# A DRAIN on GpSimd ahead of the last gather of a mixture-of-experts layer

## The chip, the cores and the metric

The kernel runs on one core of a Trainium2 chip. The metric is the device time of one execution in microseconds (us). The core has five engines with an instruction queue each: TensorE (PE in the rows; PEld is its weight load), VectorE (DVE), ScalarE (ACT), GpSimd (POOL) and SyncE (SP), and 16 DMA engines that they share. A q behind an engine's name in a row (POOLq, SPq) means an instruction that the engine's queue handles by itself, such as a wait on a semaphore, a branch or a DRAIN. Such instructions are not counted as busy time.

## The reference, cut to what matters

One layer: a gated linear attention over 512 tokens with 256 tokens of context, then a mixture of 16 experts with two experts for each token, then a norm.

```python
h2 = _modulate(_rmsnorm(x, norm2_g[i]), sh2, sc2).reshape(n_lat, D_MODEL)
f = _moe(h2, w_router, b_router, w_gate_e[i], w_up_e[i], w_down_e[i])
x = x + g2 * f.reshape(bsz, t, D_MODEL)
return _rmsnorm(x, final_g)
...
def _moe(h, w_router, b_router, w1, w3, w2):   # gates: the two best experts of the best group
    for e in range(N_EXPERTS):
        he = jax.nn.silu(h @ w1[e]) * (h @ w3[e])
        out = out + gates[:, e:e + 1] * (he @ w2[e])
    return out
```

## The kernel before

All weights are float32 and are read once, in transfers of 1 MB that SyncE issues. The attention comes first; its result x1 (512 rows of 1024) is written to a DRAM buffer `accd`, and the normed rows to `h2d`. Then the experts run one after another, in an order that the routing sets at run time. For each expert GpSimd gathers the rows of its tokens from `h2d` (an indirect DMA, `gather`, L1107), TensorE multiplies them with the expert's weights, VectorE scales the result into `y`, and GpSimd adds `y` to the rows of `accd` (an indirect DMA that accumulates, `scatter_add`, L1111). A tile whose expert may get at most 64 tokens is a `Part`, which lays 128 // w pieces of a row over the partitions.

The tail is written out by hand, from L1418 on, and its order is the order of the code on all five engines. `p_` is the expert before the last (index NE - 2), `q_` the last.

- L1425, L1426: the down product of `p_` and its scatter. This scatter is the last but one that the program may issue; the loop at L1492 has further ones, but it runs only where an expert has more rows than its tile holds, and in the profiled execution its branch is taken past it.
- L1427: the final norm's gain is laid out (TensorE, ScalarE; nothing on GpSimd). L1428, L1429: the up and gate products of `q_`.
- L1430 to L1436: SyncE loads the last weights and, by `finish_load` (L1343), the finished rows of `accd` into four tiles `y`, which needs the scatter of `p_` to have landed.
- L1437, `late_rows`: GpSimd gathers from `accd` (L1379 through L1107) the rows of the tokens of the last expert into `t.z`. It waits for the same scatter.
- L1440, `finish_half`: for two tiles at a time, the squares on ScalarE (L1346), the multiplication with the gain (L1352: tiles 0 and 2 on GpSimd, 1 and 3 on VectorE), the scaling on VectorE (L1356), and the store (L1357).
- L1442 to L1446: the down product of `q_`, its addition to the gathered rows (L1382), their norm, and `late_store`: GpSimd writes those rows straight into the output (L1394), over what `finish` stored.

Then comes what the framework adds (L1491 and L1492, and L1530, the end of the program): each engine waits for the semaphores of all DMAs, and two rounds of a barrier follow, in each of which every engine runs a DRAIN and GpSimd gathers the arrivals and lets the others go. Of what is executed before the change, only the opening barrier (L1523) and the closing ones (L1530) hold DRAINs.

GpSimd issues DMAs of two kinds in the program: plain ones (rows named DMA_DIRECT2D) and indirect ones (DMA_INDIRECT). Its instructions around the change are the two scatters at L1111, the gather at L1107, the two multiplications at L1352 and the store at L1394.

Of the kernel before, what the change touches and what calls it, by code (L numbers as in the profile page):

```python
# [32 lines left out]
def dit_kernel(ctx: ExitStack, tc: tile.TileContext, I, out):  # L33
    nc = tc.nc
    V, S, G, PE = nc.vector, nc.scalar, nc.gpsimd, nc.tensor
# [10 lines left out]
    def bank(p=None):  # L46
        p = p or pa
        return p.tile([P, 512], F32, tag="bk", name="bk")
# [633 lines left out]
    def load_unit(u, e, s, hs=None):  # L682
        t = u[s] if s in u else free.pop(0)
        if t is None:
            t = stg.tile([P, 2048], F32, tag="st", name="st")
        if s < 4:
            w, kk, v = I[("w_gate_e", "w_up_e")[s % 2]], 4, s // 2
        else:
            w, kk, v = I["w_down_e"], 2, s - 4
        w = w[0, e] if isinstance(e, int) else w[0, bass.ds(e, 1)].rearrange("a k n -> (a k) n")  # L690
        h = range(kk) if hs is None else hs
        d = nc.sync.dma_start(t.rearrange("p (k n) -> p k n", k=kk)[:, h.start:h.stop],
                              w.rearrange("(k p) n -> p k n", p=P)[:, kk * v + h.start:kk * v + h.stop])
        if len(dmas) >= 3 and not isinstance(e, int):
            back = 2 if hs is not None or len(dmas) >= 88 else 3
            tc.add_manual_dep(d.ins, dmas[-back].ins.name, mybir.DependencyInfo(mybir.DependencyClass.Sync, mybir.DependencyReason.DATA), reason="queue depth")
        dmas.append(d)
        u[s] = t
# [628 lines left out]
    def lay(name, src):  # L1327
        A = P // tiles[-1][2]
        for a in range(A):
            q, n = slice(P // A * a, P // A * (a + 1)), D // A  # L1330
            S.copy(fin[name][q, 0:n], src[q, a * n:a * n + n])

    def finish_g():
        for a in range(2):
            sl = slice(a * 512, a * 512 + 512)
            pt = bank()
            PE.matmul(pt, one, fin["row"][:, sl], start=True, stop=True)
            S.copy(fin["g"][:, sl], pt)
        lay("h", fin["g"])

    def finish_load(ts=range(4)):
        for t in ts:
            nc.sync.dma_start(fin["y"][t], accd[t * P:(t + 1) * P, :])  # L1343
# [15 lines left out]
    def finish_half(t):  # L1359
        squares(t)  # L1360
        finish_mul(t)
        if t == 0:
            finish_mul(1)
        squares(t + 1)
        finish_rsqrt(t)
        finish(t)
        finish(t + 1)
# [9 lines left out]
    def late_rows(t):  # L1377
        t.z = xbuf()[:, 0:t.n]
        gather(t.z, parts(accd, t.A), t.idx, t.A * T)  # L1379

    def late_add(t):
        V.tensor_add(t.z, t.z, t.y)  # L1382

    def late_square(t):
        S.activation(mo.tile([P, 512], BF16, tag="ohx", name="jk3", bufs=NO)[:, 0:t.n], t.z, AF.Square, accum_out=lss)

    def late_out(t):
        pt = bank(pb)
        PE.matmul(pt[:, 0:1], SELP, lss, start=True, stop=True)
        rsqrt(lrs, pt[:, 0:1], 1, 1.0 / D, "x")  # L1390
        V.scalar_tensor_tensor(t.z, t.z, lrs, fin["h"][:, 0:t.n], op0=OP.mult, op1=OP.mult)

    def late_store(t):
        G.indirect_dma_start(out=parts(out[0], t.A), out_offset=bass.IndirectOffsetOnAxis(ap=t.idx, axis=0), in_=t.z, in_offset=None,  # L1394
                             bounds_check=t.A * T - 1, oob_is_err=False)
# [24 lines left out]
    with tc.manual_schedule(engines=tail):  # L1420
        p_, q_ = ex[NE - 2:]
        p, q = p_.tls[0], q_.tls[0]
        p.late = mo.tile([P, D], F32, tag="t4", name="y", bufs=NY)[:, 0:p.n]
        q.late = fin["y15"][:, 0:q.n]
        p_.down(wts[NE - 2])  # L1425
        p_.scatter()  # L1426
        finish_g()  # L1427
        q_.up(wts[NE - 1], "a")  # L1428
        q_.up(wts[NE - 1], "b")  # L1429
        for c in "uFab":  # L1430
            if c == "F":
                finish_load()
            elif c in "0123":
                finish_load([int(c)])
            else:
                load_unit(wts[NE - 1], regs[NE - 1], {"u": 4}.get(c, 5), {"a": range(1), "b": range(1, 2)}.get(c))  # L1436
        late_rows(q)  # L1437
        q_.turn()
        S.preload_act_table_set("natural_log_exp_and_others")
        for h in range(2):  # L1440
            finish_half(2 * h)
        q_.down(wts[NE - 1])  # L1442
        late_add(q)
        late_square(q)
        late_out(q)
        late_store(q)  # L1446
# [87 lines left out]
```

## Time and profile before

| | |
|---|---|
| median of 3 runs | 674.66 us (674.36 to 675.53) |
| the profiled execution | 677.96 us |
| its span, first to last instruction | 676.2 us |
| what lies around the span | 1.76 us |
| PE, DVE, ACT, POOL busy | 617.7, 465.6, 303.6, 101.9 us |
| DMA | 170.92 MB, mean 253 GB/s |

The profile records one execution by itself, 3.3 us longer than the median of the runs. Its times count from the first instruction of the span. TensorE is busy 91% of the span, but the last six microseconds or so hold no busy engine at all; what stands there is only in the rows of the queues.

### The profile page before, as it was taken

How to read it: one execution, taken by the hardware profiler on the slowest of the kernel's cores; microseconds unless marked ns; L12 is line 12 of the kernel's file. 1: busy time of each engine (PE TensorE's matmuls, PEld its weight loads, DVE VectorE, ACT ScalarE, POOL GpSimd, SP SyncE). 2: the span in 40 equal slices, each digit the busy share in tenths (PEclk: the TensorE clock that was granted, in tenths of full speed). 3: DMA queues.
4: the chain of work that ended last, by engine and by line, in shares of the span. 5: the costliest groups of instructions: out<-in, count | busy, mean ns of one | idle time of the engine just before them, and what ended most of it. 6: DMA issues, size and time to landing. Idle time of an engine off the chain costs nothing. (4 is left out here: it accounts for less than half of the span.)

```text
span 676.2 us, 11367 instructions
## 1 busy us (share of the span) xinstructions
PE 617.7 (91%) x4260; PEld 417.3 (62%) x4260; DVE 465.6 (69%) x994; ACT 303.6 (45%) x513; POOL 101.9 (15%) x104
## 2 busy tenths in 40 slices
PE   3999999999999999999988899999999999999650
PEld 3777577767878878778773664545465667654210
DVE  5776499669958934653685796563776789999332
ACT  6334397276241416523431554323453567762240
POOL 3030000010100010104002143011212222330130
PEclk9999999999999999999989899999999999999755
DMA  8995562210336754297748899999999999999882
GB/s 277 340 353 174 194 241 63 64 64 3 127 93 223 246 188 174 88 360 251 298 143 296 329 300 369 329 337 315 328 342 371 334 348 367 373 385 337 260 317 111
DMA packets 79163, 170.92 MB, mean 253 GB/s; under 512 B 6325, under 2 KB 16875, under 8 KB 78210
## 3 DMA queue, kind: packets, MB, share of 16 engines
q1 hardware_dynamic: 71760, 156.26, 65.3%
q0 software_dynamic: 5248, 10.68, 6.8%
q10 hardware_dynamic: 2098, 3.24, 1.6%
q8 instruction: 34, 0.56, 0.3%
q14 instruction: 23, 0.19, 0.1%
HBM read 158.90 MB, written 13.09 MB: 254 GB/s over the span
## 5 line engine op out<-in xcount | busy, mean ns | idle before, releaser
L51 PE MATMUL bk<-wh,fh 128*128 128x512 f32 (+3 forms) x276 | 111.7, 412 | 1.2 <-ACT fh L56 1.2
L52 PE MATMUL bk<-wl,fh 128*128 128x512 f32 (+3 forms) x276 | 110.7, 403 | 0.0
L53 PE MATMUL bk<-wh,fl 128*128 128x512 f32 (+3 forms) x276 | 109.2, 400 | 0.0
L282 DVE TENSOR_TENSOR wl<-st,wh 128x512 fp32r<-128x512 f32 x60 | 39.9, 686 | 39.1 <-ACT wh L281 37.8
L1111 POOL DMA_INDIRECT accd<-y,gix x17 | 41.0, 2410 | 169.7 <-DVE y L1171 78.6
L56 ACT CAST wh<-su 128x1024 fp32r<-128x1024 f32 x45 | 46.8, 1049 | 42.7 <-PE bk L53 41.6
L51 PEld LDWEIGHTS bk<-wh,fh 128*128 128x128 f32 (+3 forms) x276 | 50.4, 184 | 24.0 <-issue 5.9
L281 ACT CAST wh<-st 128x512 fp32r<-128x512 f32 x60 | 35.9, 621 | 61.0 <-PE bk L53 50.8
L57 DVE TENSOR_TENSOR wl<-su,wh 128x1024 fp32r<-128x1024 f32 x45 | 54.5, 1221 | 12.3 <-ACT wh L56 9.3
L52 PEld LDWEIGHTS bk<-wl,fh 128*128 128x128 f32 (+3 forms) x276 | 50.8, 184 | 15.2 <-issue 2.4
L53 PEld LDWEIGHTS bk<-wh,fl 128*128 128x128 f32 (+3 forms) x276 | 50.5, 183 | 13.4 <-issue 1.2
L1207 PE MATMUL bk<-su,xg 128*32 128x256 f32 (+1 forms) x248 | 42.7, 503 | 5.2 <-DMA su<-in_w_up_e_dram 3.8
L1107 POOL DMA_INDIRECT xg<-h2d,gix x17 | 21.2, 1249 | 86.6 <-DMA h2d<-xg 48.9
L56 ACT CAST fx<-su 128x1024 fp32r<-128x1024 f32 x21 | 22.0, 1048 | 26.1 <-PE bk L53 25.5
L57 DVE TENSOR_TENSOR fx<-su,fx 128x1024 fp32r<-128x1024 f32 x21 | 25.7, 1222 | 11.0 <-ACT fx L56 10.8
L51 PE MATMUL bk<-fx,fh 128*128 128x512 f32 (+3 forms) x68 | 28.5, 419 | 0.1
L52 PE MATMUL bk<-fx,fh 128*128 128x512 f32 (+3 forms) x68 | 27.6, 405 | 0.8 <-DVE fx L57 0.8
L53 PE MATMUL bk<-fx,fl 128*128 128x512 f32 (+3 forms) x68 | 26.9, 396 | 0.2 <-DVE fl L57 0.2
L1207 PEld LDWEIGHTS bk<-su,xg 128*32 128x32 f32 (+1 forms) x248 | 12.1, 126 | 23.7 <-issue 16.6
L1207 PE MATMUL bk<-su,he 128*64 128x512 f32 (+1 forms) x136 | 23.1, 555 | 3.9 <-DVE he L1224 2.1
L250 POOL DMA_DIRECT2D mrd<-mrow x8 | 3.8, 484 | 130.5 <-DVE mrow L248 130.5
L1238 DVE SCALAR_TENSOR_TENSOR y<-bk,gsl,g1b 64x512 f32<-64x512 f32 (+1 forms) x16 | 10.9, 681 | 14.6 <-PE bk L1207 14.5
(478 smaller groups left out, 1318.5 us busy)
## 6 DMA issues: line engine op xcount, KB each, us to landing
su<-in_w_up_e_dram SPq DMA_DIRECT2D x23, 1024.0 KB, 9.3
su<-in_w_down_e_dram SPq DMA_DIRECT2D x21, 1024.0 KB, 8.2
su<-in_w_gate_e_dram SPq DMA_DIRECT2D x19, 1024.0 KB, 7.9
st<-in_gla_w_in_dram SPq DMA_DIRECT2D x10, 1024.0 KB, 5.3
QQ<-in_w_mod_dram SPq DMA_DIRECT2D x5, 1024.0 KB, 6.4
st<-in_w_gate_e_dram SPq DMA_DIRECT2D x5, 1024.0 KB, 7.7
st<-in_w_up_e_dram SPq DMA_DIRECT2D x5, 1024.0 KB, 7.5
B<-in_w_mod_dram SPq DMA_DIRECT2D x4, 1024.0 KB, 4.8
```

Of the source, the lines that this page charges most:

```text
L51: PE.matmul(o, ah, bh, start=first, stop=False)
L52: PE.matmul(o, ah, bl, start=False, stop=False)
L53: return PE.matmul(o, al, bh, start=False, stop=last)
L56: S.copy(hi, full)
L57: return V.tensor_sub(lo, full, hi.bitcast(F32))
L250: G.dma_start(mrd[4 * h_ + c4:4 * h_ + c4 + 1, :], mrow[32 * c4:32 * c4 + 1, :])
L281: S.copy(w[0][:, k], st[:, k])
L282: mark[0] = V.tensor_sub(w[1][:, k], st[:, k], w[0][:, k].bitcast(F32))
L1107: G.indirect_dma_start(out=xg, out_offset=None, in_=src, in_offset=bass.IndirectOffsetOnAxis(ap=idx, axis=0), bounds_check=n - 1, oob_is_e ...
L1111: G.indirect_dma_start(out=dst, out_offset=bass.IndirectOffsetOnAxis(ap=idx, axis=0), in_=y, in_offset=None, bounds_check=n - 1, oob_is_er ...
L1207: PE.matmul(o[s.w * a:s.w * a + s.w], l, r(a), start=first, stop=last, tile_position=(0, s.w * a))
L1238: s.mark = V.scalar_tensor_tensor(y[q], s.py[q], s.gs[q], g2b[q, a * s.n:a * s.n + s.n], op0=OP.mult, op1=OP.mult)
```

## The change

One line: a DRAIN instruction on GpSimd's queue, between the scatter of the expert before the last and the gather for the last expert. The DRAIN carries no wait on a semaphore and sets none. In the built program it is the only instruction that is added; nothing is removed or moved on any engine, and every other instruction waits for the same counts as before. The lines below it move down by one: L1427 is the DRAIN afterwards, the closing barrier is L1531, the branch past the loop L1493.

```diff
         p_.down(wts[NE - 2])
         p_.scatter()
+        G.drain()
         finish_g()
         q_.up(wts[NE - 1], "a")
         q_.up(wts[NE - 1], "b")
```

## Rows read from the trace of the kernel before

**Rows 1.** Busy time of each engine in four stretches at the end (from:to in us, length, busy us and number of instructions of each engine, TensorE's granted clock, the share of the DMA engines that was busy, GB/s).
```profile
639.80:647.40 7.60, 3.50 (x40) 1.48 (x36) 0.00 (x0) 0.00 (x0) 0.00 (x0) 0.72 0.91 297
647.40:656.90 9.50, 6.60 (x50) 2.04 (x42) 3.35 (x6) 5.52 (x10) 6.33 (x3) 0.50 0.89 340
666.90:669.60 2.70, 0.00 (x0) 0.00 (x0) 0.00 (x0) 0.00 (x0) 0.00 (x0) 0.50 0.08 24
669.60:675.40 5.80, 0.00 (x0) 0.00 (x0) 0.00 (x0) 0.00 (x0) 0.00 (x0) 0.50 0.00 0
```

**Rows 2.** The instructions of the program's last line, L1530 (engine, operation, count: shortest/median/longest in ns, start of the first and of the last in us).
```profile
L1530 POOLq EVENT_SEMAPHORE  x4: 17/17/17, 675.4 to 676.1; - x4
L1530 SPq DRAIN  x3: 7/7/13, 669.4 to 675.6; - x3
L1530 POOLq DRAIN  x3: 46/105/5703, 669.6 to 675.9; - x3
L1530 ACTq DRAIN  x2: 8/8/8, 669.5 to 675.6; - x2
L1530 DVEq DRAIN  x2: 10/14/17, 669.8 to 675.6; - x2
L1530 PEldq DRAIN  x2: 8/8/8, 670.0 to 675.7; - x2
```

**Rows 3.** Waits of SyncE's queue from 640 us on (who waited, for whom: us in total, times, longest).
```profile
SPq L1530 <- PEq L1530: 6.6, 2, 6.1
SPq L1343 <- DMA accd<-y,gix: 4.0, 1, 4.0
```

**Rows 4.** The program's opening, L1523, on GpSimd's queue (columns as in rows 2).
```profile
L1523 POOLq INC_SWDGE_SEM  x1: 27/27/27, 0.1 to 0.1; - x1
...
L1523 POOLq DRAIN  x1: 188/188/188, 0.3 to 0.3; - x1
```

**Rows 5.** The branch past the loop, L1492, on GpSimd's queue (columns as in rows 2).
```profile
L1492 POOLq INC_SWDGE_SEM  x1: 1575/1575/1575, 666.5 to 666.5; - x1
```

**Rows 6.** GpSimd's instructions over the whole span, by line: those that issue a DMA (count, busy us, mean ns, idle time before them and what ended it).
```profile
L1111 POOL DMA_INDIRECT accd<-y,gix x17 | 41.0, 2410 | 169.7 <-DVE y L1171 78.6 <-DVE y L1238 39.2 <-DMA accd<-y,gix 15.7
L1107 POOL DMA_INDIRECT xg<-h2d,gix x17 | 21.2, 1249 | 86.6 <-DMA h2d<-xg 48.9 <-DVE pis L1010 19.8 <-PE bk L1220 12.0
...
L234 POOL DMA_DIRECT2D mrow<-in_b_mod_dram x8 | 3.9, 506 | 33.9 <-DVE mrow L232 33.8
L250 POOL DMA_DIRECT2D mrd<-mrow x8 | 3.8, 484 | 130.5 <-DVE mrow L248 130.5
L324 POOL DMA_DIRECT2D F<-in_gla_b_gate_dram x6 | 3.1, 518 | 0.0
L323 POOL DMA_DIRECT2D F<-in_gla_w_gate_b_dram x6 | 2.9, 487 | 34.5 <-DVE F L326 33.0 <-DMA F<-in_gla_w_gate_b_dram 1.3 <-issue 0.2
...
L121 POOL DMA_DIRECT2D wga<-in_gla_w_gate_a_dram x2 | 1.9, 946 | 0.0
...
L1107 POOL DMA_INDIRECT xg<-accd,gix x1 | 1.1, 1078 | 7.6 <-DMA st<-in_w_up_e_dram 7.6
L1394 POOL DMA_INDIRECT out_dram<-xg,gix x1 | 1.1, 1057 | 9.5 <-DVE xg L1391 9.5
...
L79 POOL DMA_DIRECT2D raw<-in_b_mod_dram x1 | 0.7, 694 | 0.9 <-POOLq L1523 0.9
L80 POOL DMA_DIRECT2D raw<-in_norm_g_dram x1 | 0.6, 590 | 0.0
...
L81 POOL DMA_DIRECT2D raw<-in_gla_norm_g_dram x1 | 0.5, 523 | 0.0
```

**Rows 7.** GpSimd's instructions in order of time in the tail (start us, us, what; in brackets the idle time before, and what ended it).
```profile
638.23 1.55 POOL L1111 DMA_INDIRECT accd<-y,gix  x1 [7.83 <-DMA accd<-y,gix]
647.43 1.08 POOL L1107 DMA_INDIRECT xg<-accd,gix  x1 [7.64 <-DMA st<-in_w_up_e_dram]
650.70 2.34 POOL L1352 TENSOR_TENSOR su<-B,srg 128x1024 f32<-128x1024 f32 x1 [2.19 <-DMA B<-accd]
653.43 2.91 POOL L1352 TENSOR_TENSOR su<-su,srg 128x1024 f32<-128x1024 f32 x1 [0.38 <-DMA su<-accd]
665.79 1.06 POOL L1394 DMA_INDIRECT out_dram<-xg,gix  x1 [9.46 <-DVE xg L1391]
```

**Rows 8.** The gather's own wait on GpSimd's queue, ahead of the gather of rows 7 (columns as in rows 2).
```profile
L1107 POOLq EVENT_SEMAPHORE  x1: 8259/8259/8259, 638.1 to 638.1; - x1
```

**Rows 9.** GpSimd's three DMAs of rows 7, median us from issue to landing.
```profile
accd<-y,gix POOLq DMA_INDIRECT x1, 8.1
...
xg<-accd,gix POOLq DMA_INDIRECT x1, 5.3
...
out_dram<-xg,gix POOLq DMA_INDIRECT x1, 2.7
```

**Rows 10.** VectorE in order of time, the users of what GpSimd makes in the tail: the scaling of tiles 0 and 1, of tiles 2 and 3, the last expert's result, its addition to the gathered rows.
```profile
656.92 1.42 DVE L1356 TENSOR_SCALAR su<-su,rstd 128x1024 f32<-128x1024 f32 x2
...
660.24 1.42 DVE L1356 TENSOR_SCALAR su<-su,rstd 128x1024 f32<-128x1024 f32 x2
661.57 0.48 DVE L1232 SCALAR_TENSOR_TENSOR srg<-bk,gsl,srg 128x256 f32<-128x256 f32 x1
662.08 0.42 DVE L1382 TENSOR_TENSOR xg<-xg,srg 128x256 f32<-128x256 f32 x1
```

**Rows 11.** All executions of the scatter, L1111 (columns as in rows 2).
```profile
L1111 POOL DMA_INDIRECT accd<-y,gix x17: 1462/1902/4592, 391.7 to 638.2; - x17
```

## The prediction

> **What bounds the kernel now.** I read the end of the span first, because the added instruction stands on a queue that computes almost nothing, so that it can only matter through waits. In [rows 1] the reader sees two stretches after 666.9 us without one busy instruction on any engine; the second, 669.6 to 675.4, has no DMA traffic either. That is 5.8 us of the 676.2 us span in which nothing is computed or moved. [Rows 2] say what stands there. All engines have come to the closing barrier by 670.0 and run a DRAIN of 7 to 17 ns there, but one of GpSimd's three DRAINs takes 5703 ns. The first of the three starts at 669.6 and the next instruction of that queue, the one that collects the arrivals, at 675.4, so the long one is the first: 669.6 + 5.7 = 675.3. [Rows 3] show how easily this is missed: SyncE's 6.1 us wait at the end is put down to TensorE's queue, whose own DRAIN took 8 ns. The bound of the last 5.3 us, from 670.0 (TensorE's DRAIN, the latest of the others) to 675.3, is therefore GpSimd's DRAIN.
>
> What does it do in this time? It isn't waiting for data: the last DMA that GpSimd issued, the store, started at 665.79 [rows 7] and took 2.7 us to land [rows 9], at 668.5, over a microsecond before the DRAIN began. It isn't a price of every DRAIN on this engine: the two that follow it take 105 and 46 ns [rows 2], and the one in the opening, before GpSimd issued any DMA, 188 ns [rows 4]. What differs is what lies behind it. GpSimd issued 17 + 17 + 8 + 8 + 6 + 6 + 2 + 5 single ones = 69 DMAs in the program [rows 6], none of them followed by a DRAIN before 669.6. A second queue instruction of GpSimd has the same pattern: 27 ns in the opening [rows 4], 1575 ns behind the DMAs [rows 5]. My reading is that each DMA leaves an entry that is cleared only when a DRAIN is run: 5703 / 69 = 83 ns for each (an estimate; 80 ns if 188 ns of it is the DRAIN's own). The short DRAINs right after the long one say that what one DRAIN has cleared the next needn't.
>
> **The change part by part.** It is one instruction, without a semaphore, and nothing else is added, removed or moved.
>
> The price where it stands. Ahead of it are 67 of the 69 DMAs, all but the late gather and the store. By the estimate they take 67 x 83 ns = 5.5 us. GpSimd has room there: its scatter starts at 638.23 and ends at 639.8, the gather starts at 647.43 [rows 7], and between them its queue sits 8.26 us in the gather's wait, from 638.1 to 646.4 [rows 8], for the scatter to land: 638.23 + 8.1 [rows 9] = 646.3. The lower bound is nothing: the DRAIN works from 639.8 to 645.3, or holds on until 646.3 if it wants the scatter landed too, and the gather would have waited until 646.4 anyway; one or two queue instructions then follow later than now, for some 0.1 us. The upper bound is that its work begins only when the scatter has landed: 646.3 + 5.5 = 651.8. Now 1.1 us pass from the end of the wait to the start of the gather, so this starts at 652.9 in place of 647.43 and ends at 654.0. I take the lower end, since the work is on DMAs that landed long ago.
>
> Who waits behind it. On GpSimd are queued the gather, the two multiplications and the store [rows 7]. With the upper bound the first multiplication runs from 654.3 to 656.7 (2.34 us) and the second, 0.4 us later as now, from 657.0 to 660.0 (2.91 us). VectorE scales tile 0 from 656.92 and tile 2 from 660.24 [rows 10]: both in time by 0.2 us. The gathered rows land at 652.9 + 5.3 [rows 9] = 658.2 and are added at 662.08 [rows 10]. So even the upper bound costs nothing; the cover ends where the DRAIN ends after 652.1, and every microsecond past that is a microsecond of the time, by tiles 0 and 2. SyncE's loads of the finished rows wait for the scatter itself [rows 3], which is issued before the DRAIN; they don't move.
>
> What it saves. The closing DRAIN finds two DMAs: 2 x 83 ns, and 46 to 188 ns of its own, 0.2 to 0.35 us. It would end at 669.9, and TensorE's DRAIN at 670.0 is late next. So the barrier goes on at 670.0 in place of 675.3: **5.3 us less**. If the 1575 ns of [rows 5] shrink as well, nothing more is gained: that instruction ends at 668.1, and all queues then wait for the store's landing at 668.5.
>
> The unknown is how much of the 5703 ns is fixed once any DMA was issued. From below it is nothing. The nearest row for an upper end is the other queue instruction, which took 1575 ns [rows 5]: with 1.6 us fixed the closing DRAIN takes 1.6 + 0.2 = 1.8 us, ends at 671.4, and the gain is 3.9 us. I take the lower end, because the DRAINs of 46 to 188 ns are the same instruction. Sharing the time among the 36 indirect DMAs alone changes little: 158 ns each, two left over, and the DRAIN would end at 670.1.
>
> Two rules of the Trainium skill speak against this change. The page "VectorE: DVE Perf Modes", section "The DRAIN you can't avoid", holds the DRAINs of preamble and postamble for boilerplate of about 12 ns, constant on all five engines. The trace agrees on four engines (7 to 17 ns) and not on GpSimd (46 to 5703 ns [rows 2]). By that rule an added DRAIN is 12 ns, clears nothing, and the time stays as it is. The page "PSUM — Partial Sum Buffer", section "Engine vs sequencer instructions", has a drain wait until its engine is fully idle. By the rows GpSimd had been idle for some time at 669.6: its last instruction ended at 666.9 [rows 7], the queue's at 668.1 [rows 5], so that idleness alone doesn't explain the 5.7 us. By that rule too the new DRAIN would take nothing from the last one. Both are carried below as the first rival.
>
> **The rivals.**
> *The last DRAIN isn't shortened.* Its 5.7 us are a price of the end, or one fixed price whenever any DMA has been issued since the last DRAIN, so that the gather and the store bring it back. For it: 69 x 83 ns and 1 x 5.7 us can't be told apart from one long DRAIN. Against it: nothing else in [rows 2] is fixed, and the other queue instruction grew likewise, from 27 to 1575 ns [rows 4, 5], as work on a backlog would. The new DRAIN then takes 0.05 to 5.7 us, which the cover above hides (652.0 at the latest). Time: 674.66 us, no change. This is what both pages of the Trainium skill named above would give.
>
> *The DRAIN looks until the DMA engines are quiet.* Then the price is no backlog: 5.7 us of looking at the end, where all is quiet, and in the middle as long as weights stream. There the engines are 91% and then 89% busy up to 656.9 [rows 1]. The DRAIN would end at 656.9, the gather run from 658.0 to 659.1, the multiplications from 659.4 to 661.7 and from 662.1 to 665.0: 4.8 us later than VectorE wants tiles 0 and 2. The closing DRAIN stays. Time: 674.66 + 4.8 = 679.5 us, slower. It decides from 652.1 on. For it: GpSimd's work does stretch under load, the same scatter taking 1462 to 4592 ns [rows 11]. Against it: at the end there is no traffic at all from 669.6 on, and still 5.7 us.
>
> **How the numbers follow.** The profiled execution took 677.96 us, 1.76 us of it around the span. Its span would be 676.2 - 5.3 = 670.9 us, and it 672.7 us. The median of the runs lies 3.3 us lower, at 674.66; I take the same 5.3 us off it, since a wait in a queue has no reason to scale: **669.4 us**. Chances: the forecast with all sizes of its fixed part 0.83, the first rival 0.11, the second 0.06. The range: with 1.6 us fixed, 674.66 - 3.9 = 670.8, and the runs' scatter upwards (675.53 against 674.66) brings 671.6; downwards the whole 5.7 us could go if TensorE's arrival moved too, 674.66 - 5.7 = 669.0, and the runs' scatter (674.36) brings 668.6. I leave 0.03 of the forecast's chance outside, so the range holds 0.80 without reaching to the rivals. About 0.2%, 1.35 us, is what a measurement of this kernel can tell from no change; all sizes of the forecast are beyond it, so faster has 0.83, same 0.11 and slower 0.06.
>
> **What would show it.** Right: a DRAIN of GpSimd at the changed line of some 5.5 us or more that ends before 647; the gather at 647.4 to 647.7; the longest DRAIN of the closing line under 0.4 us (under 1.8 us with a fixed part); VectorE's L1356 rows, a line lower, at their old times; the span's last 5.8 us without a busy engine shrunk to below 1. The first rival: the closing DRAIN still 5.7 us. The second: the DRAIN ends past 652.1 and VectorE waits for GpSimd at the scaling. The forecast is wrong if a DRAIN clears nothing that a later one would have to do.

## The result and the profile after

Beside 15 runs of the kernel before (median 675.9 us, 674.4 to 679.1), 15 runs of the changed kernel have a median of 672.03 us (669.71 to 674.46). The ratio is 0.9941, 95% interval 0.9925 to 0.9957, that is 4.0 us less (3.9 between the two medians). The closing DRAIN shrinks as the prediction says, but the time lies 2.6 us above the forecast of 669.4 and just outside its range, which ended at 671.6. The profiled execution took 670.26 us, its span 668.5 us against 676.2 before.

The closing lines first. The program's last line, L1531 now (columns as in [rows 2]):

```profile
L1531 POOLq EVENT_SEMAPHORE  x4: 17/17/17, 667.7 to 668.4; - x4
L1531 SPq DRAIN  x3: 7/7/13, 667.1 to 667.9; - x3
L1531 POOLq DRAIN  x3: 46/105/213, 667.3 to 668.2; - x3
...
L1531 PEldq DRAIN  x2: 8/8/8, 667.7 to 668.1; - x2
```

The first of GpSimd's three DRAINs takes 213 ns in place of 5703 [rows 2]; the other two are what they were. It ends at 667.3 + 0.2 = 667.5 us, and TensorE's, at 667.7, is now the last to arrive. SyncE's wait on the barrier shrinks likewise, from 6.1 us [rows 3] (columns as there):

```profile
SPq L1531 <- PEq L1531: 1.2, 2, 0.7
```

The other queue instruction, INC_SWDGE_SEM in the branch past the loop, falls from 1575 ns [rows 5] to 231 ns. The longest wait on a semaphore in the same queue grows from 214 to 1781 ns in its place, until the store has landed, so that nothing is gained by it (columns as in [rows 2]):

```profile
L1493 POOLq EVENT_SEMAPHORE  x14: 17/43/1781, 663.8 to 667.1; - x14
...
L1493 POOLq INC_SWDGE_SEM  x1: 231/231/231, 664.0 to 664.0; - x1
```

The end of the span, by stages (columns as in [rows 1]). From SyncE's DRAIN to the end, with no engine busy and no DMA traffic, it is 1.4 us. The part of it between GpSimd's first DRAIN and the next instruction of that queue was 5.8 us before [rows 1] and is 0.4 now, from 667.3 to 667.7 by the rows above.

```profile
664.30:667.10 2.80, 0.00 (x0) 0.00 (x0) 0.00 (x0) 0.00 (x0) 0.02 (x1) 0.50 0.08 24
667.10:668.50 1.40, 0.00 (x0) 0.00 (x0) 0.00 (x0) 0.00 (x0) 0.00 (x0) 0.50 0.00 0
```

Now the place of the new DRAIN, on GpSimd's queue (columns as in [rows 2]), GpSimd's own instructions in order of time (as in [rows 7]), the scatter's time from issue to landing (as in [rows 9]), and SyncE's first load of the finished rows, which waits for the same scatter as the gather and so marks its landing to within 0.1 us:

```profile
L1427 POOLq DRAIN  x1: 8797/8797/8797, 636.9 to 636.9; - x1
```
```profile
637.11 1.55 POOL L1111 DMA_INDIRECT accd<-y,gix  x1 [6.12 <-DMA accd<-y,gix]
646.92 1.08 POOL L1107 DMA_INDIRECT xg<-accd,gix  x1 [8.26 <-PE bk L1207]
648.28 2.35 POOL L1352 TENSOR_TENSOR su<-B,srg 128x1024 f32<-128x1024 f32 x1 [0.28 <-DMA B<-accd]
650.71 3.22 POOL L1352 TENSOR_TENSOR su<-su,srg 128x1024 f32<-128x1024 f32 x1
663.26 1.06 POOL L1394 DMA_INDIRECT out_dram<-xg,gix  x1 [9.33 <-DVE xg L1391]
```
```profile
accd<-y,gix POOLq DMA_INDIRECT x1, 5.8
```
```profile
642.97 0.82 SPq L1343 DMA_DIRECT2D B<-accd  x2
```

The reader is to see that the DRAIN's row begins before the scatter's and ends at 636.9 + 8.8 = 645.7 us, 2.8 us after the landing at 637.11 + 5.8 = 642.9. The gather starts 4.0 us after the landing, where it started 1.1 us after it before (landing 646.3 [rows 9], gather 647.43 [rows 7]). This is neither of the two ends that the prediction gave, the landing itself and 5.5 us after it.

VectorE behind it, in order of time (as in [rows 10], with the small steps of the reciprocal root ahead of the first scaling):

```profile
649.49 2.23 DVE L1352 TENSOR_TENSOR su<-B,srg 128x1024 f32<-128x1024 f32 x1 [1.65 <-DMA B<-accd]
651.63 2.32 DVE L136 TENSOR_SCALAR rsv<-ss 128x2 f32<-128x2 f32 x1
653.87 0.15 DVE L127 TENSOR_TENSOR rst<-rstd 128x2 f32<-128x2 f32 x1
...
654.51 1.42 DVE L1356 TENSOR_SCALAR su<-su,rstd 128x1024 f32<-128x1024 f32 x2
...
657.70 1.42 DVE L1356 TENSOR_SCALAR su<-su,rstd 128x1024 f32<-128x1024 f32 x2
...
659.54 0.43 DVE L1382 TENSOR_TENSOR xg<-xg,srg 128x256 f32<-128x256 f32 x1
```

L136 works on two numbers per partition and takes 2.32 us; the next step starts when GpSimd's second multiplication ends (650.71 + 3.22 = 653.93). The kernel before has the same in the rows ahead of [rows 10]: L127 starts at 656.27, and the second multiplication ends at 653.43 + 2.91 = 656.34 [rows 7].

```profile
655.58 0.78 DVE L136 TENSOR_SCALAR rsv<-ss 128x2 f32<-128x2 f32 x1 [1.45 <-ACT srg L1346]
656.27 0.15 DVE L127 TENSOR_TENSOR rst<-rstd 128x2 f32<-128x2 f32 x1
```

So in both kernels VectorE's first scaling starts 0.6 us after the end of GpSimd's second multiplication: GpSimd's multiplications hold VectorE, which the prediction had not priced.

The two spans differ by 7.7 us, which the rows divide so: 1.1 because the scatter starts earlier (637.11 against 638.23 [rows 7]), 2.3 because it lands faster (5.8 against 8.1 us [rows 9]), -0.9 from the landing to the store (20.3 us against 19.4), and 5.2 from the store's start to the end of the span (5.2 us against 10.4). The first two belong to the executions and not to the change: a second trace of the kernel before (e5) has a landing after 6.1 us, and a third trace of the changed kernel (e9) starts this scatter at 638.02, 0.2 us from where it was before.

### The profile page after: what moved, and what is told of

Same layout as the page of the kernel before. It is cut to its first block, busy times and chain, and to the rows that moved or that the text cites. A ratio compares the mean times of both kernels' runs of the same rounds, so it can differ in the third digit from the quotient of the medians.

```text
span 668.5 us, 11368 instructions
## 1 busy us (share of the span) xinstructions
PE 615.7 (92%) x4260; PEld 417.2 (62%) x4260; DVE 467.5 (70%) x994; ACT 303.3 (45%) x513; POOL 102.1 (15%) x104
## 5 line engine op out<-in xcount | busy, mean ns | idle before, releaser
L1111 POOL DMA_INDIRECT accd<-y,gix x17 | 40.6, 2390 | 168.4 <-DVE y L1171 78.6
L57 DVE TENSOR_TENSOR wl<-su,wh 128x1024 fp32r<-128x1024 f32 x45 | 54.5, 1221 | 12.4 <-ACT wh L56 10.7
L1207 PE MATMUL bk<-su,xg 128*32 128x256 f32 (+1 forms) x248 | 40.6, 477 | 1.5 <-DVE xg L1201 1.5
L1107 POOL DMA_INDIRECT xg<-h2d,gix x17 | 21.4, 1256 | 87.6 <-DVE ohx L996 49.4
```

Source lines behind the costliest of these rows:

```text
L57: return V.tensor_sub(lo, full, hi.bitcast(F32))
L1107: G.indirect_dma_start(out=xg, out_offset=None, in_=src, in_offset=bass.IndirectOffsetOnAxis(ap=idx, axis=0), bounds_check=n - 1, oob_is_e ...
L1111: G.indirect_dma_start(out=dst, out_offset=bass.IndirectOffsetOnAxis(ap=idx, axis=0), in_=y, in_offset=None, bounds_check=n - 1, oob_is_er ...
L1207: PE.matmul(o[s.w * a:s.w * a + s.w], l, r(a), start=first, stop=last, tile_position=(0, s.w * a))
```

## The experiments

**Theories.** A: the closing DRAIN's backlog is the whole of the change, the place costs nothing, and the missing microsecond is the base and scatter of the runs. B: the close gives 5.2 us, and the place takes 1 to 2 us back, since the gather comes later and GpSimd's multiplications behind it hold VectorE. C, from e5 on: a backlog also slows the scatter's landing. Against the reading of the close stands the fixed price (one long DRAIN after any DMA). Twelve further kernels ran; each ratio is to the runs of the kernel before on the same chip, in the same series. "Landing to store" runs from SyncE's load of the finished rows (646.4 in the first trace) to the start of the last store, "close" from there to the end of the span, both from the kernel's one trace.

| run | place of the DRAIN | median us (runs) | ratio, 95% interval | closing DRAIN, ns | landing to store | close |
|---|---|---|---|---|---|---|
| before, first trace | none | 675.9 (15) | 1 | 5703 | 19.4 | 10.4 |
| the change | behind the last scatter but one | 672.03 (15) | 0.9941, 0.9925 to 0.9957 | 213 | 20.3 | 5.2 |
| e1_again | the same | 671.57 (9) | 0.9938, 0.9916 to 0.9961 | 212 | 20.2 | 5.0 |
| e9_again | the same | 669.82 (6) | 0.9910, 0.9885 to 0.9934 | 213 | 20.8 | 5.0 |
| e2_early | one scatter earlier | 669.76 (6) | 0.9903, 0.9883 to 0.9924 | 376 | 19.5 | 5.1 |
| e10_early | the same | 671.91 (7) | 0.9936, 0.9912 to 0.9959 | 376 | 19.8 | 5.1 |
| e3_late | behind both multiplications | 670.77 (6) | 0.9916, 0.9889 to 0.9943 | 131 | 20.5 | 5.0 |
| e4_twice | the change's and e2's | 669.24 (6) | 0.9903, 0.9881 to 0.9925 | 207 | 19.4 | 5.0 |
| e5_before | none | 675.78 (12) | 0.9994, 0.9980 to 1.0008 | 5703 | 19.9 | 10.4 |
| e6_mid | ahead of the routing | 672.61 (12) | 0.9960, 0.9940 to 0.9980 | 2907 | 19.2 | 7.6 |
| e7_exposed | behind the last gather | 674.66 (12) | 0.9982, 0.9963 to 1.0001 | 131 | 23.9 | 5.3 |
| e8_order | the change's, gather moved | 670.40 (6) | 0.9920, 0.9896 to 0.9945 | 213 | 18.7 | 5.3 |
| e11_best | e2's, gather moved | 671.56 (11) | 0.9943, 0.9922 to 0.9963 | 376 | 20.6 | 5.0 |
| e12_every | behind every scatter | 670.58 (6) | 0.9919, 0.9896 to 0.9943 | 205 | 21.4 | 5.4 |

**e1_again** is the changed kernel unaltered, for the spread of its runs and a second trace.

> The changed kernel once more, beside the other three on one chip. Theory A (each DMA leaves an entry, the DRAIN's place is free, and what the first timing lacks of 5.2 us is scatter of the runs): 5.2 us less than before, ratio 0.9923. Theory B (the DRAIN ends after the scatter has landed, so that the gather and GpSimd's multiplications start late and give back about 1 us): 4.0 us less, ratio 0.9940. Both: closing DRAIN 0.2 us, the new DRAIN ends 2 to 3 us after the scatter's landing.

Measured: 671.57 us, ratio 0.9938 as against 0.9941 in the result, single runs from 669.3 to 674.9 us. Both theories' ratios lie in its interval. Its trace shows the hold on VectorE more plainly (in order of time, as in [rows 10]): its multiplication of tile 1, which takes 1.22 us when GpSimd is idle, takes 5.01 us, over both of GpSimd's.

```profile
648.36 5.01 DVE L1352 TENSOR_TENSOR su<-B,srg 128x1024 f32<-128x1024 f32 x1 [1.08 <-DMA su<-accd]
```

**e2_early** puts the DRAIN one scatter earlier, into the loop, and leaves the change's place without one.

```diff
+            if i == NE - 2:
+                G.drain()
             if i:
                 ex[i - 1].scatter()
```

> The DRAIN one scatter earlier, in a pause of GpSimd of 11 us with nothing in flight towards the end but that scatter; 65 DMAs ahead of it, 4 behind. Theory A: closing DRAIN 4 x 83 ns and 0.1 us, 0.4 to 0.5 us; 5.1 us less than before, the same as e1 within 0.3 us. Theory B: closing DRAIN the same, but no late gather: 5.1 us less, and about 1 us less than e1. Rival of both (one fixed price whenever DMAs were issued): closing DRAIN 5.7 us and no gain.

Measured: 669.76 us. The closing DRAIN has four DMAs to clear, and the fixed price falls: four DMAs follow a DRAIN that ended 42 us before the end, and they don't bring 5.7 us back (columns as in [rows 2]). This DRAIN too stands behind a scatter in flight, which landed at 623.2; it ends 2.7 us after that, at 615.6 + 10.3 = 625.9, where nothing on GpSimd is due until 628.78.

```profile
L1416 POOLq DRAIN  x1: 10326/10326/10326, 615.6 to 615.6; - x1
```
```profile
L1532 POOLq DRAIN  x3: 46/105/376, 666.9 to 667.8; - x3
```

The time seemed to give the change's place a price of nearly 2 us, as theory B has it. It was six runs; see e9 and e10.

**e3_late** puts the DRAIN behind both multiplications of GpSimd, ahead of the store.

```diff
         for h in range(2):
             finish_half(2 * h)
+        G.drain()
         q_.down(wts[NE - 1])
```

> The DRAIN behind GpSimd's two multiplications, in its pause of 9.4 us ahead of the last store; 68 DMAs ahead of it, 1 behind. Nobody waits for it unless it takes over 9 us. Theory A: DRAIN 68 x 83 ns = 5.6 us, closing DRAIN 0.15 to 0.25 us, 5.3 us less than before, the same as e1. Theory B: as much, and 1 us less than e1. If the 8.8 us that the DRAIN took in the changed kernel are its true price and not a wait for the scatter, the store is near its limit and the gain smaller by up to 1 us.

Measured: 670.77 us, ratio 0.9916. The DRAIN (columns as in [rows 2]) begins its row with the second multiplication at 652.4 (in order of time, as in [rows 7]) and ends at 660.75, 5.65 us after that has ended at 655.1. 68 DMAs lie ahead of it, all landed before it could start: 83 ns each, as at the close.

```profile
L1442 POOLq DRAIN  x1: 8315/8315/8315, 652.4 to 652.4; - x1
...
L1531 POOLq DRAIN  x3: 46/104/131, 668.3 to 669.1; - x3
```
```profile
652.46 2.64 POOL L1352 TENSOR_TENSOR su<-su,srg 128x1024 f32<-128x1024 f32 x1 [0.66 <-DMA su<-accd]
664.42 1.06 POOL L1394 DMA_INDIRECT out_dram<-xg,gix  x1 [9.33 <-DVE xg L1391]
```

GpSimd had 9.3 us without work before the store, so this place hides the DRAIN with 3.7 us to spare.

**e4_twice** has both DRAINs, the change's and that of e2, so that the one in the change's place finds only two DMAs.

> Both DRAINs, that of e2 and that of the change. The second finds only two DMAs and the scatter in flight. Theory A and B: it ends within 0.3 us of the scatter's landing, so the gather starts as early as before the change; closing DRAIN 0.2 us. Theory A: 5.3 us less than before, like e1. Theory B: about 1 us less than e1. If the second DRAIN still ends 2 to 3 us after the landing, the DRAIN's length in this place isn't the backlog.

Measured: 669.24 us. The second DRAIN (queue, columns as in [rows 2]; then SyncE's load, GpSimd in order of time) still takes 4.95 us and ends at 641.1, just as SyncE's load finds the scatter landed. So this DRAIN waits for the landing, though its backlog is two entries; the gather starts 1.3 us after SyncE's load, where it is 0.7 to 1.0 us in the traces with no DRAIN there (0.7 in e2, 1.0 in before and e5).

```profile
L1429 POOLq DRAIN  x1: 4950/4950/4950, 636.2 to 636.2; - x1
```
```profile
641.07 0.82 SPq L1343 DMA_DIRECT2D B<-accd  x2
```
```profile
636.38 1.55 POOL L1111 DMA_INDIRECT accd<-y,gix  x1 [6.42 <-DMA accd<-y,gix]
642.35 1.08 POOL L1107 DMA_INDIRECT xg<-accd,gix  x1 [4.41 <-PE bk L1207]
```

**e5_before** is the kernel before, unaltered.

> The kernel before, unchanged, for a second trace and more runs of it. In the first trace its last scatter but one took 8.1 us from its row's start to its landing; with a DRAIN anywhere it took 4.9 to 6.9 us. If the 2 us are this one trace's (theory B, the close alone gains 5.2 us and the place costs up to 1 us), the landing takes 6 to 7 us here, and from the landing to the first scaling by VectorE it is 10.6 us again. If the backlog itself slows the scatter's landing (theory C, which would explain that the early DRAIN gains more than 5.2 us), it takes 8 us again. The closing DRAIN takes 5.5 to 5.9 us by both. Time 676 us, ratio 1.000 with an interval of 0.002 to 0.003 either way.

Measured: 675.78 us, 674.6 to 676.6. The closing DRAIN has its 5703 ns again, to the nanosecond. The scatter starts at 638.02 and the rows have landed at 644.13, 6.1 us later (GpSimd and SyncE in order of time). Theory C falls, and with it what the first trace's slow landing had seemed to say.

```profile
638.02 1.55 POOL L1111 DMA_INDIRECT accd<-y,gix  x1 [6.33 <-DMA accd<-y,gix]
645.16 1.08 POOL L1107 DMA_INDIRECT xg<-accd,gix  x1 [5.59 <-issue]
```
```profile
644.13 0.82 SPq L1343 DMA_DIRECT2D B<-accd  x2
```

**e6_mid** has its DRAIN in GpSimd's pause ahead of the routing, about half of the DMAs ahead of it and half behind.

```diff
         weights()
+        G.drain()
         ranked()
```

> The DRAIN stands in GpSimd's pause at about 371 to 387 us, ahead of the routing: 33 plain DMAs lie ahead of it, the 36 indirect ones and the rest behind. An equal share of 83 ns for every DMA: the closing DRAIN takes 36 x 83 ns, 3.0 us, and the time falls by 2.7 us, to 673.3 us, ratio 0.996. Shares for indirect DMAs alone (158 ns each): the closing DRAIN stays at 5.7 us and the time at 676, and the DRAIN in the pause takes under 0.3 us. Shares for plain ones alone: closing DRAIN 0.2 us or less, and the time 5.2 us less.

Measured: 672.61 us. The closing DRAIN takes 2907 ns (columns as in [rows 2]) where an equal share had been worked out at 3.0 us for 36 DMAs; shares for one kind of DMA alone fall.

```profile
L1531 POOLq DRAIN  x3: 46/109/2907, 667.1 to 670.6; - x3
```

The expectation counts 33 DMAs ahead of the DRAIN and 36 behind it. In the trace the gather for the first expert is ahead of it too (in order of time; the DRAIN's columns as in [rows 2]), so that it is 34 and 35. This gather landed 6.5 us after its start, at 373.4, and the DRAIN ends 1.4 us later, at 371.7 + 3.1 = 374.8.

```profile
366.92 1.10 POOL L1107 DMA_INDIRECT xg<-h2d,gix  x1 [49.23 <-DVE ohx L996]
```
```profile
L1401 POOLq DRAIN  x1: 3102/3102/3102, 371.7 to 371.7; - x1
```

With 131 ns for one DMA left, 213 for two, 376 for four, 2907 for 35 and 5703 for 69, each further DMA costs (5703 - 131) / 68 = 82 ns; between neighbouring sizes it is 82 as well, to the nanosecond: (2907 - 376) / 31 for indirect ones alone, (5703 - 2907) / 34 for 33 plain ones and a gather. The time follows: 2.9 us less by the medians, 2.8 by the close.

**e7_exposed** puts the DRAIN behind the last gather, where GpSimd's multiplications stand behind it and nothing hides it.

```diff
         late_rows(q)
+        G.drain()
         q_.turn()
```

> The DRAIN behind the gather of the last expert's rows, ahead of GpSimd's two multiplications, where nothing hides it. Theory B (68 entries of 83 ns, worked through from the end of the gather's row on, and VectorE waits for both multiplications with no room): the DRAIN ends some 8 us after the scatter's landing in place of the gather's end at 2 to 3 us, the first multiplication starts 3 to 3.5 us later than in the kernel before, counted from the landing, the first scaling by VectorE too, and of the 5.2 us of the close 2 us are left: 674 us, ratio 0.997. As the prediction had it (the multiplications have over 4 us of room, and the time goes up only by what the DRAIN ends after 652.1 us on the old trace's clock, 2.1 us): 673 us and the first scaling later by 2. If the DRAIN waits until the gather has landed and only then works through its entries: the first multiplication 8 us later and 679 us.

Measured: 674.66 us, ratio 0.9982 (0.9963 to 1.0001). The DRAIN's row (columns as in [rows 2]) ends at 644.1 + 9.6 = 653.6; the gather in flight landed 6.5 us after its start (issue to landing, as in [rows 9]), at 644.28 + 6.5 = 650.8. So 68 entries took 2.8 us from the landing on, 41 ns each, as in the changed kernel (2.8 us for 67). The closing DRAIN has one DMA to clear and takes 131 ns, 17.5 us after this DRAIN; e3's takes the same 131 ns for one DMA, 7.5 us after its DRAIN. So it is the DMAs that count, and not the time since the last DRAIN.

```profile
L1438 POOLq DRAIN  x1: 9574/9574/9574, 644.1 to 644.1; - x1
...
L1531 POOLq DRAIN  x3: 46/104/131, 671.1 to 672.1; - x3
```
```profile
xg<-accd,gix POOLq DMA_INDIRECT x1, 6.5
```

GpSimd and VectorE in order of time: the first multiplication waits for the DRAIN until 653.92, VectorE had been ready at 652.6 and stands 3.71 us, and then its scaling takes 3.48 us while the second multiplication runs.

```profile
644.28 1.08 POOL L1107 DMA_INDIRECT xg<-accd,gix  x1 [4.71 <-issue]
653.92 2.34 POOL L1352 TENSOR_TENSOR su<-B,srg 128x1024 f32<-128x1024 f32 x1 [8.56 <-DMA su<-in_w_down_e_dram]
656.23 2.33 POOL L1352 TENSOR_TENSOR su<-su,srg 128x1024 f32<-128x1024 f32 x1
```
```profile
652.42 0.16 DVE L129 SCALAR_TENSOR_TENSOR rstd<-rst,rstd 128x2 f32<-128x2 f32 x1
656.29 3.48 DVE L1356 TENSOR_SCALAR su<-su,rstd 128x1024 f32<-128x1024 f32 x2 [3.71 <-POOL su L1352]
...
661.55 1.42 DVE L1356 TENSOR_SCALAR su<-su,rstd 128x1024 f32<-128x1024 f32 x2
```

The expectation by theory B hit the time and not the way to it. It had the DRAIN work on from the end of the gather's instruction and the first multiplication 3 to 3.5 us late; that starts 10.7 us after SyncE's load, against 4.9 in e5. From the landing to the store it is 23.9 us in place of 19.9 in e5: 4.0 us of the 5.1 saved at the close are lost again, and 1.1 are left, by the medians 0.9, which the interval can't tell from nothing. Where the DRAIN's time is exposed, it costs time.

**e8_order** is the changed kernel with the gather behind GpSimd's first multiplication.

```diff
-        late_rows(q)
         q_.turn()
...
         finish_mul(t)
         if t == 0:
+            late_rows(q)
             finish_mul(1)
```

> The changed kernel, with the gather of the last expert's rows behind GpSimd's first multiplication. Theory B (the DRAIN ends 2.8 us after the landing, the gather's 1.1 us then push the first multiplication back by 0.3 to 0.9 us): the first multiplication starts 4.4 us after the scatter's landing, as soon as its tile is there, and the second 1.5 us later than that order allows now, since the gather stands between them; the first scaling stays where it was or comes up to 0.5 us earlier, and the time is that of the changed kernel, 671.5 us, within 0.5. If the place costs nothing (theory A): the same 671.5 us, with the first scaling where it was. A time of 670 us or less would say that the gather's place ahead of the multiplication is the whole of the 2 us by which the early DRAIN is better.

Measured: 670.40 us, landing to store 18.7. Taken alone it would say that the gather's place is worth over a microsecond. **e11_best** has the same order with the DRAIN of e2, which by theory B should have been the best of all.

> The early DRAIN, and the gather of the last expert's rows behind GpSimd's first multiplication, with no DRAIN between scatter and gather. Theory B (GpSimd's multiplications hold VectorE's chain, and the gather ahead of them costs up to 1 us): the first multiplication starts with the landing of its tile, 3.4 to 4.5 us after the scatter's, landing to store 18.7 us as in the kernel with the other order, and 6 us less than before: 669.7. If the multiplications have room (theory A): as the early one, landing to store 19.5 us.

Measured: 671.56 us (11 runs), landing to store 20.6. What e8 showed is not repeated; of the places where the DRAIN is hidden, neither order nor place is worth more here than executions differ.

**e9_again** and **e10_early** repeat e1 and e2 side by side.

> The changed kernel once more, beside the early DRAIN on the same chip: over two calls the change took 4.3 us off and the DRAIN one scatter earlier 6.1 us, while the traces give 0.6 to 1 us between them (from the scatter's landing to the end of the span 25.3 and 25.5 us against 24.6). Theory B (the place costs what the traces show): 671.2 us, 4.5 less than before, within 0.7, and 0.6 to 1 us above the early one. If the place costs 2 us by something ahead of the landing: 671.5 and 2 us above.

> The early DRAIN once more (between the two scatters ahead of the last but one). Theory B: 670.3 us, 5.4 less than before, within 0.7; the closing DRAIN 0.38 us; landing to the end of the span 24.6 us. If the place costs 2 us: 669.6.

Measured: 669.82 and 671.91 us, the other way round than in the first series. Theory B's 2 us fall. Over all its runs the change has ratios of 0.9941, 0.9938 and 0.9910 (30 runs), the early DRAIN 0.9903 and 0.9936 (13 runs): weighted by runs 0.9934 and 0.9921, 4.5 and 5.3 us, to about 0.8 and 1.1 us by their intervals.

**e12_every** puts a further DRAIN behind every scatter of the loop.

```diff
             if i:
                 ex[i - 1].scatter()
+                G.drain()
```

> The changed kernel with a further DRAIN behind every scatter of the loop: 15 DRAINs, each with a few DMAs ahead of it, straight behind an indirect DMA. If a DRAIN only works through entries of 83 ns from the end of the scatter's row on, all but the first take 1.5 + 0.2 to 0.5 us. If it starts only when the rest of the scatter's own work is done (theory B's reading of the 0.5 to 3.2 us that the DRAINs behind an indirect DMA took beyond their entries, and none in the quiet place), they take 2.0 to 5 us, as the second one of the kernel with two did (4.95). If it waits until the scatter has landed, 5 to 8 us. The last one ends with or ahead of the landing, the closing DRAIN takes 0.2 us, and the time is as the early DRAIN's, 670 us, unless the DRAINs in the loop hold up the gathers for later experts: then above it.

Measured: 670.58 us. The fourteen DRAINs of the loop (columns as in [rows 2]) take 6.8 to 15.9 us, and the kernel's scatters take 6.5 to 13.2 us from issue to landing:

```profile
L1417 POOLq DRAIN  x14: 6840/9392/15894, 391.3 to 629.4; - x14
```
```profile
L1111 POOL DMA_INDIRECT accd<-y,gix x17: 1461/2121/4592, 392.5 to 637.1; - x17
...
DMA to landing us min/median/max: 6.5/8.8/13.2
```

The shortest and the median DRAIN are longer than the shortest and the median landing by 0.3 and 0.6 us; 0.2 of that is the head start of the DRAIN's row over the scatter's (636.2 against 636.38 in e4). The longest is the first, with the whole backlog of the program's start: 391.3 + 15.9 = 407.2, 1.5 us after the landing of its scatter (392.5 + 13.2 = 405.7). The last one in the loop ends at 629.4 + 6.8 = 636.2 with one entry, as its scatter lands (629.6 + 6.5 = 636.1). The readings that a DRAIN works only on its entries, or waits only for the scatter's own work, are refuted; it waits for the landing. The time is no worse for it: what comes behind a scatter on GpSimd in the loop isn't late by it.

## Why the prediction missed

**What held.** The closing DRAIN takes what a backlog of one entry for each DMA that GpSimd issued since its last DRAIN would take: 83 ns for each forecast, 82 measured over five sizes; 0.2 to 0.35 us forecast for the close, 0.21 measured. TensorE's DRAIN is late next, INC_SWDGE_SEM shrinks and gives nothing. The close gives 5.3 us by the forecast, 5.2 by the traces (10.4 to 5.2). Both rivals are dead: the first by the 213 ns, the second since the DRAIN ended at 645.7 while the DMA engines were busy throughout (columns as in [rows 1]; the share from 645 to 647 us is 1.01).

```profile
645.00:647.00 2.00, 1.53 (x10) 0.40 (x4) 0.00 (x0) 0.37 (x1) 0.08 (x1) 0.50 1.01 346
```

**The step that failed on the chip** is "I take the lower end, since the work is on DMAs that landed long ago". The DRAIN wants the last scatter landed, and half of its work, 41 ns for an entry, comes after that: 2.8 us. The true value lies half way between the ends. The step behind it was wrong too: "even the upper bound costs nothing" compared the multiplications with the scalings that use their tiles, and overlooked that while GpSimd multiplies, VectorE's steps ahead of the scaling are held. The second multiplication's end sets the first scaling in the kernel before already, so that the room of some 4 us (from 656.34, where that multiplication ends, to 660.24 [rows 10]) was none. What it costs is small, since the first multiplication waits for its tile as well. Counted from SyncE's load, the gather starts 3.95 us later in all three traces of the changed kernel and takes 1.08, so that the first multiplication cannot start before 5.0 us. In the eight traces that keep the order of the code and have no long DRAIN in the gather's way (before, e2, e3, e4, e5, e6, e10, e12) it started 3.9 to 6.4 us after the load, 4.7 in the mean, and 5.3 if each of them below 5.0 is raised to it. That is some 0.5 us, an estimate from these rows, and landing to store is 20.4 us in the mean of the changed kernel's three traces against 19.9 in those eight, which range from 19.2 to 21.4. 5.2 - 0.5 = 4.7 us is near the 4.5 that the 30 runs give. The gather's delay of 2.9 us is shown by all three traces; that it costs 0.5 us of time is argued from them, and the runs can't settle it, with 4.5 against 5.3 us and about 1 us on each.

**The other half of the miss** is the base and the range. The forecast was 674.66 - 5.3 from three runs; 15 runs of the same kernel have 675.9, and in the later series 675.9, 675.5 and 675.3. That is 1.2 of the 2.6 us. The other 1.4 are the gain, 3.9 us between these medians in place of 5.3: some 0.5 of it by the estimate above, the rest scatter as far as the runs show, since the same kernel gave 4.3 and 5.5 us in the other series. Neither the base nor the place takes the forecast out of its range by itself, nor do both: 669.4 + 1.2 + 0.5 = 671.1 us. It needed the scatter of the result's own runs on top. "The runs' scatter" was taken from 674.36 to 675.53, while single runs of one kernel spread over 5 us and more (669.3 to 674.9 in e1). A range that reached 1.2 us further for the base, to 672.8, would have held the result.

## What to carry to other kernels

In this kernel GpSimd pays 82 ns at the close for each DMA that it issued, where no engine counts as busy, unless a DRAIN stands earlier; where a closing DRAIN is as long, try one where GpSimd is without work for as long as the backlog takes (some 6 us here) and no indirect DMA is in flight, such as behind the multiplications. Between a scatter and what waits for it, it waits for the landing and works on after it. Here the runs can't tell the hidden places apart; only the exposed one (e7) lost most of the gain. Price an instruction that may wait by all it may wait for, and take the base from as many runs as the difference needs: three runs with a spread of 1.2 us hid one of 5 us.

## What the runs showed of the hardware

- GpSimd's DRAIN behind an indirect DMA in flight ends after that DMA has landed: 0.1 us later with two entries (e4), 1.4 with 34 (e6), 2.8 with 67 (the change) and with 68 (e7), 41 ns for each. With all landed before it starts, an entry costs 82 to 83 ns (e3, the close). So half of its work is done while it waits; which half isn't shown.
- INC_SWDGE_SEM at the close has the same kind of backlog, which a DRAIN clears: 231 ns with two DMAs left, 895 with 35 (e6), 1575 with 69, (1575 - 231) / 67 = 20 ns for each.
- While GpSimd multiplies two tiles in SBUF, VectorE's instructions stretch: 5.01 us for one of 1.22 (e1), 2.32 us for one on two columns (the change). The Trainium skill, page "SBUF — State Buffer", section "SBUF: two separate sides", says that the two engines share a pair of ports under an exclusive lock, that a VectorE instruction with two SBUF inputs takes part in it, and that whichever starts first has the pair for its whole instruction while the other is blocked. The first row agrees: L1352 has two inputs in SBUF, and it ends at 653.37, 1.1 us after GpSimd's second multiplication (652.28). What holds the second row isn't shown.
- The scatter's landing differs between executions of one kernel by 2 us (8.1 and 6.1 us, before and e5), and whole runs by 5.6 us (e1) and 6.4 us (e11).
